# Full-row low products in the attention scores, and new byte positions for the token parts

## The chip, the cores and the metric

The kernel runs on one core of a Trainium2 chip. The metric is the device time of one execution in microseconds. Weights come from HBM, everything between stays in SBUF and PSUM.

## The reference

Two layers work on 512 tokens of 1024 channels: 256 latent tokens x and 256 context tokens ctx. Each layer is a feed-forward half, a token mixing and a second feed-forward half, each behind an RMS norm with shift and scale from a conditioning vector. In the second layer the context is needed only up to the keys and values of the mixing.

```
x = x + 0.5 * gate1 * SwiGLU(mod(rmsnorm(x)))            # ctx too; d_ff = 2816
x = x + gate2 * W_out( sum_b sigmoid(G_b) * P_b(branch_b) )   # ctx too in layer 0
x = x + 0.5 * gate3 * SwiGLU(mod(rmsnorm(x)))            # ctx too in layer 0
# branches of one input projection: A attention (4 heads, 2 key heads), B a gated
# linear recurrence in both directions, C pooled means, D attention in a 2-D window
# A and D:  s = q @ k.T / 8 ; p = softmax(s) ; o = p @ v      (head size 64)
```

All inputs and the result are float32.

## The kernel before

Tokens lie along the free dimension: `x` is a tile of 128 partitions by 8 chunks by 512 tokens (latents are columns 0 to 255, context 256 to 511).

**Products in parts.** A float32 product is made of three products of `fp32r` parts. A weight unit (128 x 1024) is loaded by SyncE as `raw`; ScalarE rounds it to `whi` (L74), VectorE takes the rest `wlo` (L77). The tokens are split the same way: `apply` (L346) writes the normed tokens as `xh` on ScalarE (L355) and `xl` on VectorE (L356), by way of a tile `nt` (L352). `mm3` (L94) then issues for each of 8 chunks k three matmuls into one PSUM bank: whi with xh (L102), whi with xl (L103), wlo with xh (L104); the weights are stationary and the tokens stream past. `group` (L106) does the same for several units at once. The hidden activations of a feed-forward half are parts `hh`, `hl`, the merged branches `mh`, `ml`, one branch `bh`, `bl`.

**Stages.** The program is one long list: feed-forward 1 of layer 0 (starts cold, `cold_units` L446), mixing of layer 0, feed-forward 2 of layer 0, feed-forward 1 of layer 1, mixing of layer 1, feed-forward 2 of layer 1. All products have 512 columns up to the mixing of layer 1, apart from the first units of a stage and the last two output units, which go in halves of 256 columns; from the mixing of layer 1 on nearly all have 256 columns. A unit of the gate and up projections (`pg`, `pu`) or of the mixing (`proj`, `gate`) is 24 matmuls, one of the down projection (`pd`) 33. The first units of a stage wait for `apply`; in the last stage `early_units` (L426) takes products of tokens that are not yet divided by their norm, kept in the context's half of `xh` (columns 256 to 511) with the shift in two columns more (512 and 513).

**Where the parts lie.** `xh` and `xl` are tiles of 8 x 514 columns (L146, L147), so chunk k starts 2056 bytes behind chunk k-1. In the compiled program xh starts at byte 36,032 of each partition and xl at 52,480: by lines of 128 bytes xh's chunk k starts at byte 64 + 8k of its line, xl's at byte 8k. `hh`, `hl` start at byte 64 of a line in every chunk (pitch 2048 bytes), `mh`, `ml` at byte 32 in layer 0 and 64 in layer 1. The weights start at byte 0 of a line in the pool that lasts (four buffers of `whi` and of `wlo`); units that a stage keeps in its own pool (the chunk c = 2 of a feed-forward half, the last two output units) lie at byte 64, in the mixing of layer 0 at byte 32.

**Scores.** `score_parts` (L637) makes for each of the two heads h of a pair a tile `qs` with the rounded q in the head's own 64 rows and again in the other 64, and `ks` with the rounded k in the own rows and its rest in the others. `attend` (L657) then needs two matmuls per head and 128 queries: qs with ks over 128 rows (L700), and for the rest of q, `ql`, over the head's own 64 rows (L701, one tile for both heads). 32 such pairs have 512 columns and 16 have 256. A tile framework orders the instructions of all generators and puts in the waits; on each engine they run in that order.

Of the kernel before, what the change touches and what calls it, by code (L numbers as in the profile page):

```python
# [17 lines left out]
P = 128  # L18
# [25 lines left out]
    0, 72, 80, 88, 96, 104, 105, 106, 107, 109, 117)  # L44

# [6 lines left out]
class Net:  # L52
# [41 lines left out]
    def mm3(self, ps, w, xh, xl, ks, c0, c1, first=True, last=True, k0=0):  # L94

        nc = self.nc
        hi, lo = w
        n = len(ks)
        for j, k in enumerate(ks):
            wh = hi[:, (k0 + j) * P:(k0 + j + 1) * P]  # L100
            wl = lo[:, (k0 + j) * P:(k0 + j + 1) * P]
            nc.tensor.matmul(ps, wh, xh[:, k, c0:c1], start=first and j == 0, stop=False)  # L102
            nc.tensor.matmul(ps, wh, xl[:, k, c0:c1], start=False, stop=False)  # L103
            nc.tensor.matmul(ps, wl, xh[:, k, c0:c1], start=False, stop=last and j == n - 1)  # L104

    def group(self, ws, pss, c0, c1, mid=iter(()), ks=range(NK), marks=(3, 5)):  # L106

        nc = self.nc
        for k in ks:
            if k in marks:  # L110
                next(mid, None)
            a, b = self.xh[:, k, c0:c1], self.xl[:, k, c0:c1]
            for (hi, lo), ps in zip(ws, pss):
                w = slice(k * P, (k + 1) * P)
                nc.tensor.matmul(ps, hi[:, w], a, start=k == 0, stop=False)
                nc.tensor.matmul(ps, lo[:, w], a, start=False, stop=False)
                nc.tensor.matmul(ps, hi[:, w], b, start=False, stop=k == NK - 1)
# [10 lines left out]
    def consts(self):  # L128
        nc, cp, i = self.nc, self.cp, self.i
        self.x = cp.tile([P, NK, TT], F32, name="x")  # L130
        self.cv = cp.tile([P, NK, 2], F32, name="cv")
# [14 lines left out]
        self.xh = cp.tile([P, NK, TT + 2], F32R, name="xh")  # L146
        self.xl = cp.tile([P, NK, TT + 2], F32R, name="xl")  # L147
# [13 lines left out]
        for k in range(NK):  # L161
            for r in range(2):
                sq = self.tp.tile([P, T], F32, tag="nt" if r else "sq", name="sq")
                x = self.x[:, k, r * T:(r + 1) * T]
                if r:
                    nc.vector.tensor_tensor(out=sq, in0=x, in1=x, op=ALU.mult)
                else:
                    nc.scalar.activation(sq, x, AF.Square)
                nc.tensor.matmul(ps[r], self.ones, sq, start=k == 0, stop=k == NK - 1)
        self.rstd = {r: self.tp.tile([P, T], F32, tag="rstd", name="rstd") for r in range(2)}  # L170
        for r in range(2):
            nc.scalar.activation(self.rstd[r], ps[r], AF.Sqrt, scale=1.0 / D, bias=self.eps)
            nc.vector.reciprocal(self.rstd[r], self.rstd[r])

# [17 lines left out]
    def bounds(self, pool):  # L192
# [4 lines left out]
        m = pool.tile([P, 4], F32, name="lbm")  # L197
# [148 lines left out]
    def apply(self, g, sh, r, ks=range(NK)):  # L346
# [21 lines left out]
    def early(self, l):  # L368
# [5 lines left out]
        hi = self.xh[:, :, TT:TT + 2]  # L374
        nc.scalar.copy(hi, sh)
        nc.vector.tensor_tensor(out=self.xl[:, :, TT:TT + 2], in0=sh, in1=hi.bitcast(F32), op=ALU.subtract)
# [49 lines left out]
    def early_units(self, ws, l, hp, hh, hl):  # L426
# [4 lines left out]
        self.group(ws, [p[:, :T + 2] for p in pss], T, TT + 2, self.stat_steps(0), marks=(1, 3))  # L431
        g = self.gain(l, 7, C_N2)
        self.apply(g, self.mods(l, 6), 0)
        for c in range(2):
            s, u = (hp.tile([P, TT], F32, tag="sg", bufs=2, name="sg") for _ in range(2))
            b = self.tp.tile([P, 2], F32, tag="eb", name="eb")
            for j, t in enumerate((s, u)):
                ps = pss[2 * c + j]
                nc.vector.tensor_copy(b[:, j:j + 1], ps[:, T:T + 1])
                nc.vector.tensor_tensor(out=t[:, :T], in0=ps[:, :T], in1=self.rstd[0], op=ALU.mult)  # L440
# [5 lines left out]
    def cold_units(self, wgu, hp, evac):  # L446
# [44 lines left out]
        hh, hl = (hp.tile([P, FH, TT], F32R, tag=t, name=t) for t in ("hh", "hl"))  # L491
# [5 lines left out]
    def ffn(self, l, wgu, wd, col, mods, segs, rate=0, whole=False, cold=False):  # L497
# [3 lines left out]
        gate = None  # L501
        with tc.tile_pool(name=f"ffn{col}_{l}", bufs=1) as hp:
            self.apool, self.rate = hp, rate
# [7 lines left out]
            for f in range(2):  # L511
                c = 0
                if cold and f == 0:
                    hh, hl = self.cold_units(wgu[l], hp, evac)
                    c = 2
                    self.steady = True
                else:
                    hh, hl = (hp.tile([P, FH, TT], F32R, tag=t, name=t) for t in ("hh", "hl"))
# [118 lines left out]
    def score_parts(self, pool, q, k, n, ks=None):  # L637
# [4 lines left out]
        ql = pool.tile([P, TT], F32R, tag="ql", name="ql")  # L642
# [3 lines left out]
        for h in range(2):  # L646
# [7 lines left out]
            nc.vector.tensor_tensor(out=ql[own, :n], in0=q[own, :n], in1=qs[h][own, :n].bitcast(F32), op=ALU.subtract)  # L654
        return qs, ql, ks

    def attend(self, pool, tmp, first, second, v, n, bias, bo):  # L657
# [7 lines left out]
        for i in range(len(items) + 2):  # L665
# [24 lines left out]
            if i < len(items):  # L690
# [5 lines left out]
                for h in range(2):  # L696
                    rows = slice(64 * h, 64 * h + 64)
# [3 lines left out]
                    nc.tensor.matmul(sc[:, :w], ql[rows, qc], ks[h][rows, k0:], start=False, stop=True)  # L701
# [111 lines left out]
    def mix(self, l, segs):  # L813
# [3 lines left out]
        cols = self.cols[l]  # L817
        with tc.tile_pool(name=f"mix{l}", bufs=1) as mp:
# [401 lines left out]
```

## Time and profile before

| | |
|---|---|
| median of 3 runs | 2163.44 us (2162.93 to 2164.12) |
| profiled execution | 2163.93 us, its span 2162.2 us |
| TensorE (PE) busy | 2140.1 us, 99%, 12446 matmul records |
| weight loads (PEld) | 1810.7 us, 84% |
| VectorE (DVE), ScalarE (ACT), GpSimd (POOL) | 66%, 42%, 2% |
| granted TensorE clock | 0.998 of 2.4 GHz |
| HBM | 136 GB/s over the span |

A matmul's row gives its start and a modelled length; consecutive matmuls overlap in it, so the pace is read from start to start, not from the length. A float32 matmul (not fp32r) has two records.

### The profile page before, as it was taken

To read this page: it belongs to the slowest core of one execution; us is meant where nothing else is said; L and a number is where in the kernel's file an instruction comes from. 1 tells how busy PE (TensorE), PEld (TensorE's weight loads), DVE (VectorE), ACT (ScalarE), POOL (GpSimd) and SP (SyncE) were. 2 spreads that over 40 slices of the span, in tenths; PEclk is the share of its full clock that TensorE was granted. 3 is DMA by queue.
4 is the path that set the end of the run, shared out by engine and by line. 5 is a ranking of instruction groups with operands and counts; after the bars stand their busy time and mean duration, and the time that the engine had idled before them with its cause. 6 is when DMAs were issued, how large, how long until landed. Compare 5 with 4: busy or idle time off the path is not lost.

```text
span 2162.2 us, 31602 instructions
## 1 busy us (share of the span) xinstructions
PE 2140.1 (99%) x12446; PEld 1810.7 (84%) x12446; DVE 1437.7 (66%) x2355; ACT 905.9 (42%) x1488; POOL 33.0 (2%) x79
## 2 busy tenths in 40 slices
PE   8999999999999999999999999999999999999998
PEld 5777777988787778888787888878789899999998
DVE  5987986676366454676676667567665867677555
ACT  4332333546446433433232344223334665656443
POOL 0000000000000000000000000000000000000000
PEclk9999999999999999999999999999999999999999
DMA  7655654221222222343454344445433233355553
GB/s 297 215 173 186 206 183 134 92 95 50 69 70 78 73 88 88 115 148 127 138 185 152 116 134 147 137 138 179 147 119 115 103 111 112 120 184 184 170 197 114
DMA packets 89509, 296.71 MB, mean 137 GB/s; under 512 B 10256, under 2 KB 12176, under 8 KB 89360
## 3 DMA queue, kind: packets, MB, share of 16 engines
q1 hardware_dynamic: 89360, 294.69, 40.3%
q8 instruction: 98, 1.61, 0.3%
q14 instruction: 51, 0.42, 0.1%
HBM read 293.60 MB, written 1.05 MB: 136 GB/s over the span
## 4 chain that ended last, share of the span: by engine, by line
PE 95%; DVE 2%; ACT 2%; issue 1%; DMA 0%; DVEq 0%; ACTq 0%; SPq 0%
PE pg L102 6%; PE pu L102 6%; PE pu L103 6%; PE pg L103 6%; PE pu L104 6%; PE pg L104 6%; PE pd L102 6%; PE pd L104 6%; PE pd L103 6%; PE gate L102 4%; PE gate L103 4%; PE gate L104 4%; PE proj L103 2%; PE proj L102 2%; PE proj L104 2%; PE blev L747 2%
## 5 line engine op out<-in xcount | busy, mean ns | idle before, releaser
L74 ACT CAST whi<-raw 128x1024 fp32r<-128x1024 f32 (+2 forms) x444 | 430.4, 972 | 907.1 <-PE pu L103 216.5
L77 DVE TENSOR_TENSOR wlo<-raw,whi 128x1024 fp32r<-128x1024 f32 (+2 forms) x444 | 498.6, 1124 | 331.0 <-ACT whi L74 327.6
L264 DVE SCALAR_TENSOR_TENSOR aacc<-araw,sil,aacc 128x512 f32<-128x512 f32 x448 | 312.4, 746 | 89.1 <-DMA araw<-in_wada 88.6
L102 PE MATMUL pg<-xh,whi 128*128 128x512 f32 (+1 forms) x640 | 235.4, 368 | 0.3 <-DVE sg L440 0.3
L102 PE MATMUL pu<-xh,whi 128*128 128x512 f32 (+1 forms) x640 | 235.1, 367 | 0.0
L103 PE MATMUL pu<-xl,whi 128*128 128x512 f32 (+1 forms) x640 | 235.0, 367 | 0.0
L103 PE MATMUL pg<-xl,whi 128*128 128x512 f32 (+1 forms) x640 | 234.9, 367 | 0.0
L104 PE MATMUL pu<-xh,wlo 128*128 128x512 f32 (+1 forms) x640 | 234.5, 366 | 0.0
L104 PE MATMUL pg<-xh,wlo 128*128 128x512 f32 (+1 forms) x640 | 234.5, 366 | 0.0
L102 PE MATMUL pd<-hh,whi 128*128 128x512 f32 (+1 forms) x616 | 226.4, 368 | 0.0
L104 PE MATMUL pd<-hh,wlo 128*128 128x512 f32 (+1 forms) x616 | 225.2, 366 | 0.0
L103 PE MATMUL pd<-hl,whi 128*128 128x512 f32 (+1 forms) x616 | 225.2, 366 | 0.0
L102 PE MATMUL gate<-xh,whi 128*128 128x512 f32 (+1 forms) x512 | 176.6, 345 | 0.0
L103 PE MATMUL gate<-xl,whi 128*128 128x512 f32 (+1 forms) x512 | 173.7, 339 | 0.0
L104 PE MATMUL gate<-xh,wlo 128*128 128x512 f32 (+1 forms) x512 | 173.4, 339 | 0.0
L102 PEld LDWEIGHTS pg<-xh,whi 128*128 128x128 f32 x640 | 120.6, 188 | 23.7 <-issue 2.0
L102 PEld LDWEIGHTS pu<-xh,whi 128*128 128x128 f32 x640 | 120.6, 188 | 23.2 <-issue 2.0
L104 PEld LDWEIGHTS pg<-xh,wlo 128*128 128x128 f32 x640 | 120.7, 189 | 20.9
L104 PEld LDWEIGHTS pu<-xh,wlo 128*128 128x128 f32 x640 | 120.7, 189 | 20.8
L103 PEld LDWEIGHTS pu<-xl,whi 128*128 128x128 f32 x640 | 120.5, 188 | 20.6
L103 PEld LDWEIGHTS pg<-xl,whi 128*128 128x128 f32 x640 | 120.5, 188 | 20.4
L102 PEld LDWEIGHTS pd<-hh,whi 128*128 128x128 f32 x616 | 115.7, 188 | 22.5 <-issue 2.2
(275 smaller groups left out, 3804.3 us busy)
## 6 DMA issues: line engine op xcount, KB each, us to landing
raw<-in_wgu SPq DMA_DIRECT2D x176, 512.0 KB, 3.3
araw<-in_wada SPq DMA_DIRECT2D x128, 512.0 KB, 3.2
raw<-in_wgate SPq DMA_DIRECT2D x64, 512.0 KB, 3.2
raw<-in_wd SPq DMA_DIRECT2D x64, 384.0 KB, 3.0
raw<-in_win SPq DMA_DIRECT2D x44, 512.0 KB, 3.3
raw<-in_wd SPq DMA_DIRECT2D x64, 320.0 KB, 2.8
aspace<-in_wada SPq DMA_DIRECT2D x16, 512.0 KB, 9.0
raw<-in_wbr SPq DMA_DIRECT2D x16, 512.0 KB, 3.4
```

The source lines that it names most:

```text
L74: nc.scalar.copy(hi, src)
L77: nc.vector.tensor_tensor(out=lo, in0=src, in1=hi.bitcast(F32), op=ALU.subtract)
L102: nc.tensor.matmul(ps, wh, xh[:, k, c0:c1], start=first and j == 0, stop=False)
L103: nc.tensor.matmul(ps, wh, xl[:, k, c0:c1], start=False, stop=False)
L104: nc.tensor.matmul(ps, wl, xh[:, k, c0:c1], start=False, stop=last and j == n - 1)
L264: nc.vector.scalar_tensor_tensor(out=acc[r], in0=w[:, j], scalar=c, in1=acc[r], op0=ALU.mult, op1=ALU.add)
L747: nc.tensor.matmul(ps[:, g * P:(g + 1) * P], k[:, h, g * P:(g + 1) * P], x[:, h, (g ^ cross) * P:((g ^ cross) + 1) * P], start=True, stop= ...
```

## The change

Four edits. (1) `xh` and `xl` become views of one tile `xs`; `place`, called at the head of each stage, sets them: 112 bytes into a line of 128 for both, 16,512 bytes apart, for the stages with 512 columns, and for the last two stages 64 bytes into a line, 18,432 bytes apart. The pitch of a chunk is 2048 bytes now. The two shift columns of `early_units` move into the last two columns of the latents' half. (2) `hidden` places `hh`, `hl` at byte 112 of a line (64 in the last stage), and a pad of 64 bytes heads the feed-forward pool. With it the weights that this pool holds move from byte 64 of a line to byte 0. `lbm` leaves the mixing's pool, whose tiles in layer 0 move from byte 32 to byte 0. (3) `ql` becomes one tile per head, its other 64 rows set to zero by GpSimd, and L701 runs over all 128 rows. (4) `nt` is one buffer of 512 columns, used in halves, in place of two of 256; the second `ql` lies in it too, and so do the squares of the context's half at the start.

```diff
+LINE = 32
+PLACES = {(0, C_N1): (28, NK * TT + LINE, (28, 12)), (0, C_NM): (28, NK * TT + LINE, None),
+          (0, C_N2): (28, NK * TT + LINE, (28, 12)), (1, C_N1): (28, NK * TT + LINE, (28, 12)),
+          (1, C_NM): (16, NK * TT + TT, None), (1, C_N2): (16, NK * TT + TT, (48, 0))}
...
+        self.xs = cp.tile([P, 2 * NK * TT + TT + LINE], F32R, name="xs")
-        self.xh = cp.tile([P, NK, TT + 2], F32R, name="xh")
-        self.xl = cp.tile([P, NK, TT + 2], F32R, name="xl")
...
-                sq = self.tp.tile([P, T], F32, tag="nt" if r else "sq", name="sq")
+                sq = self.tp.tile([P, TT], F32, tag="nt", bufs=1, name="sq")[:, :T] if r else self.tp.tile(
+                    [P, T], F32, tag="sq", name="sq")
...
+    def place(self, l, phase):
+        h, d, o = PLACES[l, phase]
+        self.xh, self.xl = (self.xs[:, a:a + NK * TT].rearrange("p (k t) -> p k t", t=TT) for a in (h, h + d))
+        return o
...
-        m = pool.tile([P, 4], F32, name="lbm")
+        m = self.tp.tile([P, 4], F32, tag="rs", name="lbm")
...
-        for k in ks:
-            t = self.tp.tile([P, T], F32, tag="nt", name="nt")
+        for j, k in enumerate(ks):
+            if j % 2 == 0:
+                pair = self.tp.tile([P, TT], F32, tag="nt", bufs=1, name="nt")
+            t = pair[:, j % 2 * T:j % 2 * T + T]
...
-        hi = self.xh[:, :, TT:TT + 2]
+        hi = self.xh[:, :, T - 2:T]
...
-        self.group(ws, [p[:, :T + 2] for p in pss], T, TT + 2, self.stat_steps(0), marks=(1, 3))
+        self.group(ws, [p[:, :T + 2] for p in pss], T - 2, TT, self.stat_steps(0), marks=(1, 3))
...
+    def hidden(self, hp, off):
+        return tuple(hp.tile([P, FH * TT + pad], F32R, tag=t, name=t)[:, a:a + FH * TT].rearrange(
+            "p (f t) -> p f t", t=TT) for t, pad, a in zip(("hh", "hl"), (48, 16), off))
...
+        off = self.place(l, col)
         with tc.tile_pool(name=f"ffn{col}_{l}", bufs=1) as hp:
+            hp.tile([P, LINE // 2], F32, name="pad")
...
-                    hh, hl = (hp.tile([P, FH, TT], F32R, tag=t, name=t) for t in ("hh", "hl"))
+                    hh, hl = self.hidden(hp, off)
...
-        ql = pool.tile([P, TT], F32R, tag="ql", name="ql")
+        ql = [pool.tile([P, TT], F32R, tag="ql", name="ql"), self.tp.tile([P, TT], F32R, tag="nt", bufs=1, name="ql")]
+        for h in range(2):
+            nc.gpsimd.memset(ql[h][64 - 64 * h:128 - 64 * h, :n].bitcast(F32), 0.0)
...
-                    nc.tensor.matmul(sc[:, :w], ql[rows, qc], ks[h][rows, k0:], start=False, stop=True)
+                    nc.tensor.matmul(sc[:, :w], ql[h][:, qc], ks[h][:, k0:], start=False, stop=True)
...
+        self.place(l, C_NM)
         with tc.tile_pool(name=f"mix{l}", bufs=1) as mp:
```

The edits in `mm3` and `group` name the same operands in another way and change no instruction.

## Rows read from the trace of the kernel before

**Rows 1.** The page: busy time of the matmul engine, and the chain by engine.

```profile
PE 2140.1 (99%) x12446; PEld 1810.7 (84%) x12446; DVE 1437.7 (66%) x2355; ACT 905.9 (42%) x1488; POOL 33.0 (2%) x79
...
PE 95%; DVE 2%; ACT 2%; issue 1%; DMA 0%; DVEq 0%; ACTq 0%; SPq 0%
```

**Rows 2.** Groups by line with shapes apart: shape, count, busy us, mean ns, idle before.

```profile
L102 PE MATMUL pg<-xh,whi 128*128 128x512 f32 x480 | 190.1, 396 | 0.0
...
L102 PE MATMUL pd<-hh,whi 128*128 128x512 f32 x462 | 183.9, 398 | 0.0
```

**Rows 3.** Timeline, PE, one unit of 512 columns: start us, length us, line, operation.

```profile
340.78 0.39 PE L102 MATMUL pu<-xh,whi 128*128 128x512 f32 x1
...
342.41 0.40 PE L103 MATMUL pu<-xl,whi 128*128 128x512 f32 x1
342.65 0.40 PE L104 MATMUL pu<-xh,wlo 128*128 128x512 f32 x1
...
344.98 0.39 PE L102 MATMUL pu<-xh,whi 128*128 128x512 f32 x1
...
345.67 0.39 PE L102 MATMUL pu<-xh,whi 128*128 128x512 f32 x1
...
346.13 0.39 PE L104 MATMUL pu<-xh,wlo 128*128 128x512 f32 x1
```

**Rows 4.** Timeline, PE, a down unit of 512 columns, first and last of 33.

```profile
354.60 0.40 PE L102 MATMUL pd<-hh,whi 128*128 128x512 f32 x1
...
362.07 0.40 PE L104 MATMUL pd<-hh,wlo 128*128 128x512 f32 x1
```

**Rows 5.** Timeline, PE, last stage, a down unit of 256 columns, first and last of 33.

```profile
2042.12 0.28 PE L102 MATMUL pd<-hh,whi 128*128 128x256 f32 x1
...
2045.75 0.28 PE L104 MATMUL pd<-hh,wlo 128*128 128x256 f32 x1
```

**Rows 6.** Timeline, PE, last stage, a unit with weights at byte 64, first and last of 33.

```profile
2143.01 0.28 PE L102 MATMUL last<-hh,whi 128*128 128x256 f32 x1
...
2146.85 0.28 PE L104 MATMUL last<-hh,wlo 128*128 128x256 f32 x1
```

**Rows 7.** Timeline, PE, output unit of the second mixing, first and 21st matmul.

```profile
1938.47 0.28 PE L102 MATMUL po<-mh,whi 128*128 128x256 f32 x1
...
1940.83 0.28 PE L104 MATMUL po<-mh,wlo 128*128 128x256 f32 x1
```

**Rows 8.** Timeline, PE, units of 256 columns, first and last of 24: gate, then pu.

```profile
1899.35 0.28 PE L102 MATMUL gate<-xh,whi 128*128 128x256 f32 x1
...
1902.07 0.28 PE L104 MATMUL gate<-xh,wlo 128*128 128x256 f32 x1
...
2018.47 0.29 PE L102 MATMUL pu<-xh,whi 128*128 128x256 f32 x1
...
2021.24 0.28 PE L104 MATMUL pu<-xh,wlo 128*128 128x256 f32 x1
```

**Rows 9.** Timeline, PE, a score pair of 512 columns and what follows it.

```profile
496.52 0.48 PE L700 MATMUL s<-ks,qs 128*128 128x512 f32 x1
496.93 0.50 PE L701 MATMUL s<-ks,ql 64*128 64x512 f32 x1
497.37 0.50 PE L102 MATMUL gate<-xh,whi 128*128 128x512 f32 x1
```

**Rows 10.** Groups by line with shapes apart, GpSimd.

```profile
L738 POOL MEMSET bqz<- 64x512 f32 x32 | 17.0, 531 | 580.4 <-DVE xl L356 368.5 <-PE blev L747 149.1 <-PE bo L808 35.0
```

**Rows 11.** Timeline, VectorE, the last square of the start.

```profile
13.04 0.43 DVE L166 TENSOR_TENSOR sq<-x 128x256 f32<-128x256 f32 x1 [0.44 <-PE stat L169]
```

**Rows 12.** Timeline around the end of `early_units`: VectorE's pairs of chunks, PE's next unit.

```profile
1971.91 0.87 DVE L352 SCALAR_TENSOR_TENSOR nt<-x,gain,rstd 128x256 f32<-128x256 f32 x2
...
1973.77 0.88 DVE L352 SCALAR_TENSOR_TENSOR nt<-x,gain,rstd 128x256 f32<-128x256 f32 x2
...
1975.19 0.36 PE L102 MATMUL pg<-xh,whi 128*128 128x256 f32 x1 [0.26 <-DVE sg L440]
```

More of the change, by code (lines that the diff above doesn't have):

```diff
@@ L101, in mm3 @@
             wl = lo[:, (k0 + j) * P:(k0 + j + 1) * P]
-            nc.tensor.matmul(ps, wh, xh[:, k, c0:c1], start=first and j == 0, stop=False)
-            nc.tensor.matmul(ps, wh, xl[:, k, c0:c1], start=False, stop=False)
-            nc.tensor.matmul(ps, wl, xh[:, k, c0:c1], start=False, stop=last and j == n - 1)
+            a, b = xh[:, k, c0:c1], xl[:, k, c0:c1]
+            nc.tensor.matmul(ps, wh, a, start=first and j == 0, stop=False)
+            nc.tensor.matmul(ps, wh, b, start=False, stop=False)
+            nc.tensor.matmul(ps, wl, a, start=False, stop=last and j == n - 1)
     def group(self, ws, pss, c0, c1, mid=iter(()), ks=range(NK), marks=(3, 5)):
@@ L113, in group @@
             for (hi, lo), ps in zip(ws, pss):
[L114 to L117, printed above, removed]
+                wh, wl = hi[:, k * P:(k + 1) * P], lo[:, k * P:(k + 1) * P]
+                nc.tensor.matmul(ps, wh, a, start=k == 0, stop=False)
+                nc.tensor.matmul(ps, wl, a, start=False, stop=False)
+                nc.tensor.matmul(ps, wh, b, start=False, stop=k == NK - 1)
     def warm(self, func, after):
@@ L373, in early @@
         sh = self.mods(l, 6)
-        hi = self.xh[:, :, TT:TT + 2]
+        hi = self.xh[:, :, T - 2:T]
         nc.scalar.copy(hi, sh)
-        nc.vector.tensor_tensor(out=self.xl[:, :, TT:TT + 2], in0=sh, in1=hi.bitcast(F32), op=ALU.subtract)
+        nc.vector.tensor_tensor(out=self.xl[:, :, T - 2:T], in0=sh, in1=hi.bitcast(F32), op=ALU.subtract)
         return g
@@ L438, in early_units @@
                 ps = pss[2 * c + j]
[L439 to L440 removed]
+                nc.vector.tensor_copy(b[:, j:j + 1], ps[:, 0:1])
+                nc.vector.tensor_tensor(out=t[:, :T], in0=ps[:, 2:T + 2], in1=self.rstd[0], op=ALU.mult)
             nc.scalar.activation(s[:, :T], s[:, :T], AF.Silu, bias=b[:, 0:1])
@@ L513, in ffn @@
                 if cold and f == 0:
-                    hh, hl = self.cold_units(wgu[l], hp, evac)
+                    hh, hl = self.cold_units(wgu[l], hp, evac, off)
                     c = 2
@@ L517, in ffn @@
                 else:
-                    hh, hl = (hp.tile([P, FH, TT], F32R, tag=t, name=t) for t in ("hh", "hl"))
+                    hh, hl = self.hidden(hp, off)
                 while c < FH:
@@ L653, in score_parts @@
                 nc.vector.tensor_tensor(out=ks[h][other], in0=k[own], in1=ks[h][own].bitcast(F32), op=ALU.subtract)
-            nc.vector.tensor_tensor(out=ql[own, :n], in0=q[own, :n], in1=qs[h][own, :n].bitcast(F32), op=ALU.subtract)
+            nc.vector.tensor_tensor(out=ql[h][own, :n], in0=q[own, :n], in1=qs[h][own, :n].bitcast(F32), op=ALU.subtract)
         return qs, ql, ks
```

3 lines of the change are left out of this document (1 added, 2 removed).

## The prediction

> **What bounds the kernel now.** I read the page first: the matmul engine is busy 99% of the span, and the chain that ended last runs through it for 95% [rows 1]. So the time is a sum of paces: so many products, each by the distance from its start to the next one's start. The length in a row is no pace: the 512-column products of [rows 2] have a mean length of 396 to 398 ns and overlap. I then read paces from the timeline, unit by unit, and set each beside the byte at which its operands start (the section on the kernel gives the bytes). The reader is to see five of them.
>
> - 512 columns of token parts: first to last of 24 in 5.35 us, 23 steps, 232.6 ns [rows 3]. Inside the unit the steps differ. Chunk 6 (xh at byte 112, xl at 48) takes 0.69 us for its three, 230 ns each; the step that begins with xl at byte 16 takes 0.24 us.
> - 512 columns of hidden parts, all at byte 64: 7.47 us for 32 steps, 233.4 ns [rows 4].
> - 256 columns of hidden parts, all at byte 64, weights at byte 0: 3.63 us for 32 steps, 113.4 ns [rows 5]. The same parts with weights at byte 64: 3.84 us, 120.0 ns [rows 6].
> - 256 columns of merged parts, again 64 and 0: 2.36 us for 20 steps, 118.0 ns [rows 7]. So one placement can run at two paces, 113.4 and 118.0.
> - 256 columns of token parts, bytes changing with the chunk: gate 2.72 us for 23 steps, 118.3 ns; pu 2.77 us, 120.4 ns [rows 8].
>
> The last place to read is the scores. From the start of a full-row product to that of its half-row partner pass 0.41 us, and from there to the next product 0.44 us [rows 9], where two ordinary 512-column products would take 0.47.
>
> **The change part by part.** The sum is made against the profiled execution's 2163.93 us (span 2162.2 and 1.7 around it), which is 0.5 above the median.
>
> *Token parts of 512 columns at byte 112.* By the code 24 products a unit: 120 gate and up units with 24 each (2880, six times the 480 of [rows 2]), four cold units (96), 32 gate units and 15 projections of the first mixing (768 and 360): 4104. No row has both parts at 112. The nearest is chunk 6 of [rows 3], 230 ns among neighbours at other bytes. Below it I set twice the 113.4 of [rows 5], 226.8 ns, as the floor: the smallest pace that a steady run of equal bytes shows, doubled for twice the columns. Above it stands 233.4 [rows 4], a steady run of 512 columns at byte 64. I take 227.5, near the floor, since in [rows 5] the steady run is below every mixed one of [rows 8], and chunk 6 is the lowest part of the mixed unit. 4104 x (232.6 - 227.5) = 20.9 us; ends 23.8 and -3.3.
>
> *Hidden parts of 512 columns at byte 112.* 462 products a line [rows 2] by three lines, 1386. 1386 x (233.4 - 227.5) = 8.2 us; ends 9.1 and 0.
>
> *Weights of the stage's pool at byte 0.* 396 output products of the three wide halves (12 units by 33), 120.0 now [rows 6], then 256 columns at byte 112 between 113.4 and 118.0; with 116: 1.6 us (0.8 to 2.6). 66 of the last stage go to 113.4: 0.4. 96 of the first mixing: 0.3 (0 to 0.6).
>
> *Token parts of 256 columns at byte 64.* They then lie as the hidden parts of [rows 5] and the merged parts of [rows 7] do, in lines and in weights; the distance between the parts is a multiple of 2048 bytes in all three. So 113.4 or 118.0. Last stage: 1056 products (44 units of 24), 120.4 now [rows 8]; undisturbed, so I take 114.5: 6.2 us (2.5 to 7.4). Second mixing: 1104 products (32 gate, 9 projection and 5 first units), 118.3 now; attention breaks in between, 115.5: 3.1 us (0.3 to 5.4). Halves in the earlier stages, 528 at byte 112, 118.3 to 116: 1.2 us (0 to 2.6). 144 products of 512 columns in the second mixing go to 233.4: -0.1.
>
> A rule speaks against these three parts. The Trainium skill, "TensorE: Matmul & The Clock Gate", section "Step-by-step: what each phase is for", says that the engine reads weights and streaming operand through two independent ports, so that loading the next weights takes nothing from the running product. By it the bytes would not matter. This trace disagrees: the same hidden parts run at 113.4 or 120.0 ns with the weights alone moved [rows 5, 6]. What the rule would give is a rival below.
>
> *Full-row low products.* A pair costs 0.85 us now [rows 9] and two like products then 0.47: 0.38 us. The code has 32 pairs of 512 columns and 16 of 256; what is exposed is not the streaming, so I use 0.38 for all: 48 x 0.38 = 18.2 us at most. The lower end is the half-row product's own excess, 0.44 - 0.23, by 48: 10. I take 16, for some of the time saved will be spent in waits on softmax that the engine meets sooner. What it costs: 16 zero fills on GpSimd of the size of [rows 10], 0.53 us each, on an engine that is busy 2% [rows 1]. They run beside ScalarE's copies of q into qs, which wait for the same score products to free their buffers. Behind them on GpSimd stand the recurrence's zero fills of [rows 10]; if each were late by 0.53 us and PE waited for it, 8.5 us would go.
>
> The same page of the Trainium skill, section "The mechanism" (of row and column tiling), says that a weight load runs ahead of a running product only where the row groups differ. By it the half-row products of the two heads could run beside each other, and full rows would lose that. The row shows the reverse: 0.41 and 0.44 us on either side of the half-row product [rows 9], nothing beside it.
>
> *One `nt` buffer.* `apply` works in pairs of chunks (x2 in [rows 12]): two nt, two xh, two xl, then the next two, whose VectorE writes stand in order behind the xl of the pair before. One buffer of two halves keeps that order: 0. At the start the context's squares lose their second buffer. Each of eight then waits for PE and takes its 0.43 us [rows 11] where it ran ahead: 3.4 us at most; PE has the latents' square to work on meanwhile and later waits for loads, so I take 0.5.
>
> *Shift columns in the latents' half.* `apply` now overwrites columns that `early_units` still reads, so chunk k waits for the products of chunk k. `apply` writes two chunks per 1.86 us [rows 12], and its last pair is written when the group is ending anyway: 0. If the wait were for the whole group, four pairs would stand in line behind it, 7.4 us, before PE's next unit at 1975.19.
>
> Sum: 20.9 + 8.2 + 1.6 + 0.4 + 0.3 + 6.2 + 3.1 + 1.2 - 0.1 + 16 - 0.5 = 57.3 us. 2163.9 - 57.3 = 2106.6; on the median's footing 2106.
>
> **The rivals.**
> - *512 columns keep the steady 233.4 at any byte* [rows 4]. For it: 64 and 32 are the only bytes with long steady runs of that width, and the former shows this pace. Against: chunk 6 of [rows 3]. The first two terms become -3.3 and 0, the rest stays 28.2: 2139.
> - *The byte does nothing at all,* as the ports rule would have it; only scores and start remain, 15.5 us: 2148. Against: [rows 5, 6].
> - *The scores' time turns into waits* for softmax or the recurrence. For it: DVE and ACT are busy 66% and 42% on the whole [rows 1] and the recurrence is a serial chain through them. Against: PE's chain is 95% its own. 57.3 - 16: 2123.
> - *Byte 112 locks into a slow pattern.* [rows 5] and [rows 7] show that equal bytes run in a steady pattern that repeats, good or bad; a byte can show 0.24 us in one step [rows 3]. At 240 ns for all 512-column products the first two terms turn into 4104 x 7.4 + 1386 x 6.6 = 39.5 us lost, against 28.2 won elsewhere: slower, 2175. It decides from 5.1 ns above today's mean of 232.8, that is from 237.9 ns (28.2 us by 5490 products).
> - *The parts don't lie where it says.* xs must start at a line of 128 bytes; by the compiled program x starts at byte 16,512 and takes 16,384, so xs follows at a line. Were it off, the first rival's time would hold.
>
> **How the numbers follow.** Forecast 0.66, steady 233.4 (and parts misplaced) 0.14, no effect of the byte 0.05, scores into waits 0.08, slow pattern 0.07. All terms at their good end are worth 70 us: 2093; a pace under the floor would go below. The range 2088 to 2142 takes in the forecast, the waits and the steady 233.4 and leaves out the other two, 0.12, and some of the tails. Changes under 0.2% (4.3 us) can't be told from none here. Faster 0.93 (all but the slow pattern), within 0.2% 0.01, slower 0.06.
>
> **What would show it.** A pu unit of the first stages with 23 steps in 5.23 us (227.5) in place of 5.35, and a down unit with 32 in 7.28; in the last stage pu in 2.63; the last output units at 113.4 in place of 120.0; score pairs 0.47 from first start to the next product, all on 128 rows; nothing new in PE's waits at 1975. Wrong would be: units at 233 or more, score pairs followed by idle PE, or a gap before the first unit behind `early_units`.

## The result, and the profile after

The changed kernel takes 2151.8 us in the median of four executions (2145.98 to 2152.58) against 2163.31: ratio 0.994, interval 0.9923 to 0.9958. It is faster by 11.5 us where 57 were forecast, and outside the range. The profiled execution took 2152.58 us, its span 2150.8, 11.4 under the span before. One execution of experiment 1 ran at a mean granted clock of 0.594, took 3530.24 us, and is left out below.

Line numbers have moved: `mm3` is L110 to L112 (was L102 to L104), scores L724 and L725, `apply` L368 to L372. The page after; the rows of before are [rows 1].

```profile
PE 2117.5 (98%) x12446; PEld 1809.5 (84%) x12446; DVE 1440.8 (67%) x2355; ACT 904.6 (42%) x1488; POOL 39.5 (2%) x95
...
PE 94%; DVE 3%; ACT 2%; issue 1%; DMA 0%; DVEq 0%; ACTq 0%; SPq 0%
```

PE's busy time fell by 22.6 us, but the span by 11.4: PE now stands idle where it did not. The paces are read from start to start, as before. First come a down unit of 512 columns in the second feed-forward (to be set beside [rows 4]) and a pu unit of 512 columns of the same stage (beside [rows 3]).

```profile
1086.53 0.39 PE L110 MATMUL pd<-hh,whi 128*128 128x512 f32 x1
...
1093.78 0.39 PE L112 MATMUL pd<-hh,wlo 128*128 128x512 f32 x1
...
1122.64 0.40 PE L110 MATMUL pu<-xs,whi 128*128 128x512 f32 x1
...
1128.04 0.39 PE L112 MATMUL pu<-xs,wlo 128*128 128x512 f32 x1
```

The down unit takes 7.25 us for 32 steps, 226.6 ns: the forecast's floor. The pu unit takes 5.40 for 23, 234.8 ns, more than the 232.6 before. Both kinds of part start at byte 112 of a line. In blocks of 256 bytes they do not lie alike: xs starts at byte 32,896, so xh lies at 33,008, byte 240 of 256, and xl at 49,520, byte 112. `hh` lies at 132,208, byte 112, and `hl` at 154,864, byte 240. From here on, "240/112" names the byte of the high and the low part in a block of 256.

A score pair ([rows 9]): 0.31 us to the low product and 0.23 from there, 0.54 where it was 0.85.

```profile
495.60 0.48 PE L724 MATMUL s<-ks,qs 128*128 128x512 f32 x1
495.91 0.39 PE L725 MATMUL s<-ks,ql 128*128 128x512 f32 x1
496.14 0.39 PE L724 MATMUL s<-ks,qs 128*128 128x512 f32 x1
```

In the last stage, at 192/192, pu and pd units run at 2.71 us for 23 steps and 3.77 for 32, both 117.8 ns. Before, the pu units were at 120.4 ([rows 8]) and the pd units at 113.4, with the same bytes as now ([rows 5]).

```profile
1990.27 0.28 PE L110 MATMUL pu<-xs,whi 128*128 128x256 f32 x1
...
1992.98 0.28 PE L112 MATMUL pu<-xs,wlo 128*128 128x256 f32 x1
...
2015.71 0.28 PE L110 MATMUL pd<-hh,whi 128*128 128x256 f32 x1
...
2019.48 0.28 PE L112 MATMUL pd<-hh,wlo 128*128 128x256 f32 x1
```

The largest single loss is at the start. PE's waits (engine, line, what it waited for: us in total, times, longest):

```profile
PE mm L123 <- ACT xs L371: 8.2, 3, 5.1
...
PE s L724 <- ACT bad L802: 1.8, 4, 0.7
...
PE pt L711 <- ACT ap L736: 1.5, 2, 1.2
```

The first was 2.6 us before. VectorE's timeline shows why: after the change one chunk at a time, scale (L368), a wait for ScalarE's copy, subtract (L372), then the next.

```profile
34.91 0.48 DVE L368 SCALAR_TENSOR_TENSOR nt<-x,gain,rstd 128x256 f32<-128x256 f32 x1
35.97 0.48 DVE L372 SCALAR_TENSOR_TENSOR xs<-nt,mod,xs 128x256 fp32r<-128x256 f32 x1 [0.58 <-ACT xs L371]
36.49 0.48 DVE L368 SCALAR_TENSOR_TENSOR nt<-x,gain,rstd 128x256 f32<-128x256 f32 x1
...
65.26 0.68 DVE L531 TENSOR_TENSOR sg<-sg,mm 128x512 f32<-128x512 f32 x1
```

The same place before, two at a time:

```profile
30.73 0.88 DVE L352 SCALAR_TENSOR_TENSOR nt<-x,gain,rstd 128x256 f32<-128x256 f32 x2
31.79 0.89 DVE L356 SCALAR_TENSOR_TENSOR xl<-nt,mod,xh 128x256 fp32r<-128x256 f32 x2 [0.18 <-ACT xh L355]
...
55.24 0.68 DVE L508 TENSOR_TENSOR sg<-sg,mm 128x512 f32<-128x512 f32 x1
```

The first hidden chunk is made at 65.26 us, before at 55.24: 10.0 us. PE's longest idle time, 5.14 us before 57.98, brings a second cost: its granted clock. Windows of the changed kernel (us from:to, length, busy of PE, PEld, DVE, ACT, POOL, granted clock, DMA share, GB/s):

```profile
52.00:55.00 3.00, 0.84 (x4) 0.36 (x2) 3.00 (x9) 0.51 (x1) 0.00 (x0) 1.00 0.42 134
55.00:57.00 2.00, 0.00 (x0) 0.00 (x0) 2.00 (x4) 0.00 (x0) 0.00 (x0) 0.89 0.41 131
57.00:63.30 6.30, 5.32 (x13) 4.16 (x14) 6.30 (x13) 2.64 (x4) 0.00 (x0) 0.50 0.57 196
```

After that idle time the work goes on at 0.50, 1.2 GHz, until about 63 us; before the change the clock was 1.00 (2.4 GHz) there. The 12 steps from 57.98 to 63.27 us take 5.29 us, where 512-column products go at 0.23 us each behind them: about 2.5 us, an estimate, are lost by the clock. It stood at 0.50 once before, from 25.9 to 29.2 us, behind an idle time of 2.30 us.

Where the 11.4 us come from, as sums of start-to-start times by stage and kind: scores -14.5, hidden parts of 512 columns -8.3, merged and branch parts of the first mixing -1.9, second mixing -2.0, token parts of the last stage -2.3, weights of the stage's pool -0.8; against them the start +10.0, token parts of 512 columns +4.0, hidden parts of the last stage +1.9, waits on softmax +1.0, early units +0.8. That makes -12.1, 0.7 more than the span shows; the rest is spread over small groups.

### The profile page after: what moved, and what is told of

Its sections match the earlier page's. It is cut to its first block, busy times and chain, and to the rows that moved or that the text cites. A ratio compares the mean times of both kernels' runs of the same rounds, so it can differ in the third digit from the quotient of the medians.

```text
span 2150.8 us, 31652 instructions
## 1 busy us (share of the span) xinstructions
PE 2117.5 (98%) x12446; PEld 1809.5 (84%) x12446; DVE 1440.8 (67%) x2355; ACT 904.6 (42%) x1488; POOL 39.5 (2%) x95
## 4 chain that ended last, share of the span: by engine, by line
PE 94%; DVE 3%; ACT 2%; issue 1%; DMA 0%; DVEq 0%; ACTq 0%; SPq 0%
PE pg L110 6%; PE pu L110 6%; PE pu L112 6%; PE pg L112 6%; PE pu L111 6%; PE pg L111 6%; PE pd L110 6%; PE pd L112 6%; PE pd L111 6%; PE gate L110 4%; PE gate L112 4%; PE gate L111 4%; PE proj L110 2%; PE proj L111 2%; PE proj L112 2%; PE blev L771 2%
## 5 line engine op out<-in xcount | busy, mean ns | idle before, releaser
L110 PE MATMUL pg<-xs,whi 128*128 128x512 f32 (+1 forms) x640 | 238.0, 372 | 0.8 <-DVE sg L456 0.8
L110 PE MATMUL pu<-xs,whi 128*128 128x512 f32 (+1 forms) x640 | 237.9, 372 | 0.0
L111 PE MATMUL pu<-xs,whi 128*128 128x512 f32 (+1 forms) x640 | 235.1, 367 | 0.0
L111 PE MATMUL pg<-xs,whi 128*128 128x512 f32 (+1 forms) x640 | 235.1, 367 | 0.0
L112 PE MATMUL pg<-xs,wlo 128*128 128x512 f32 (+1 forms) x640 | 234.8, 367 | 0.0
L112 PE MATMUL pu<-xs,wlo 128*128 128x512 f32 (+1 forms) x640 | 234.8, 367 | 0.0
L112 PE MATMUL pd<-hh,wlo 128*128 128x512 f32 (+1 forms) x616 | 224.3, 364 | 0.0
L110 PE MATMUL pd<-hh,whi 128*128 128x512 f32 (+1 forms) x616 | 223.8, 363 | 0.0
L110 PE MATMUL gate<-xs,whi 128*128 128x512 f32 (+1 forms) x512 | 175.0, 342 | 0.0
L112 PE MATMUL gate<-xs,wlo 128*128 128x512 f32 (+1 forms) x512 | 173.0, 338 | 0.0
L111 PE MATMUL gate<-xs,whi 128*128 128x512 f32 (+1 forms) x512 | 172.2, 336 | 0.0
L110 PEld LDWEIGHTS pg<-xs,whi 128*128 128x128 f32 x640 | 120.9, 189 | 23.4 <-issue 2.0
L112 PEld LDWEIGHTS pu<-xs,wlo 128*128 128x128 f32 x640 | 121.4, 190 | 22.2
L112 PEld LDWEIGHTS pg<-xs,wlo 128*128 128x128 f32 x640 | 121.4, 190 | 22.2
L110 PEld LDWEIGHTS pu<-xs,whi 128*128 128x128 f32 x640 | 120.9, 189 | 22.3 <-issue 2.0
L111 PEld LDWEIGHTS pu<-xs,whi 128*128 128x128 f32 x640 | 121.2, 189 | 21.0
L111 PEld LDWEIGHTS pg<-xs,whi 128*128 128x128 f32 x640 | 121.2, 189 | 20.8
L110 PEld LDWEIGHTS pd<-hh,whi 128*128 128x128 f32 x616 | 116.3, 189 | 19.5 <-issue 2.2
```

The source lines that it names most:

```text
L110: nc.tensor.matmul(ps, wh, a, start=first and j == 0, stop=False)
L111: nc.tensor.matmul(ps, wh, b, start=False, stop=False)
L112: nc.tensor.matmul(ps, wl, a, start=False, stop=last and j == n - 1)
```

## The experiments

**1. The chains of the cold start.** In `cold_units`, `apply` is called with one chunk, and each call takes a whole pair buffer. The edit hands it one half of a shared buffer; the part of the edit inside `apply`, which uses that half, is not shown.

```diff
...
             for k in (2 * j, 2 * j + 1):
+                pair = self.tp.tile([P, TT], F32, tag="nt", bufs=1, name="nt")
                 for r in range(2):
-                    self.apply(gain, mod, r, (k,))
+                    self.apply(gain, mod, r, (k,), pair[:, r * T:r * T + T])
```

> The changed kernel with one edit in cold_units: the two halves of one nt tile go to r = 0 and r = 1 of the same chunk, so that the two chains of scale, copy and subtract overlap as in the kernel before. Theory A (each one-chunk apply takes a whole pair buffer, so the chains stand in line and the first stage starts late): the pairs come back as nt x2 and xs x2 on VectorE, the first evacuation (65.26 us after the change, 55.24 before) comes at 56 to 57.5, 1.5 us of the old gap staying with the squares, and the run is 7.5 to 9 us under the changed kernel's 2151.8: 2143 to 2144.5. Rival B (the start is late because of loads or of the weight splits that share VectorE): the evacuation stays at 64 to 65 and the time within 2 us of 2151.8.

Measured: 2138.34, 2143.78 and 2144.93 us, ratio 0.9896 (0.9876 to 0.9915). Profile against profile, both with the last stage at 117.8 ns, 2143.78 against 2152.58: 8.8 us. VectorE's timeline:

```profile
32.57 0.88 DVE L369 SCALAR_TENSOR_TENSOR nt<-x,gain,rstd 128x256 f32<-128x256 f32 x2
33.63 0.88 DVE L373 SCALAR_TENSOR_TENSOR xs<-nt,mod,xs 128x256 fp32r<-128x256 f32 x2 [0.18 <-ACT xs L372]
...
57.73 0.68 DVE L533 TENSOR_TENSOR sg<-sg,mm 128x512 f32<-128x512 f32 x1
```

The pairs are back and PE's wait for xs is 1.4 us in place of 8.2. Theory A holds; the first hidden chunk, at 57.73, is still 2.5 late, and the clock's fall behind 57 us is gone.

**2. The token parts 128 bytes further, and both at byte 0.** In `PLACES`, for the four stages with 512 columns, from 240/112 to 112/240; the other kernel has `(32, NK * TT, ` there, 0/0:

```diff
-PLACES = {(0, C_N1): (28, NK * TT + LINE, (28, 12)), (0, C_NM): (28, NK * TT + LINE, None),
+PLACES = {(0, C_N1): (60, NK * TT + LINE, (28, 12)), (0, C_NM): (60, NK * TT + LINE, None),
...
```

> The changed kernel with one number changed: in the four wide stages the token parts start 128 bytes later in xs. The high part goes from byte 240 to byte 112 of a 256-byte block and the low part from 112 to 240, the distance of 129 lines of 128 bytes stays. Theory A (the pace hangs on which half of a 256-byte block the part used by two of three products starts in; the hidden parts, high at 112 and low at 240, run at 226.6 ns): the 512-column units of token parts go from 234.6 ns to 226.6 to 228; about 3000 products of the three FFNs by 7.5 ns and 1100 of the first mixing by 5.5 make 28 us, so 2123 to 2125. Rival B (the distance between the parts decides, 177 lines in the hidden parts): they stay at 234.6 and the time at 2151 to 2153. Rival C (eight chunks and 24 products against eleven and 33 make the pattern): stays too.

> The changed kernel with the token parts of the four wide stages both at byte 0 of a 256-byte block, 128 lines apart, as the merged parts of the first mixing lie (226.7 ns). Theory A (the half of the 256-byte block of the high part decides): 226.7 to 228 ns in the 512-column units, 2123 to 2125, like the run with the parts swapped; the 256-column products may move between 113.4 and 118. Rival B (the distance of 129 lines is what is slow): 226.7 here too, and not in the run with the parts swapped. Rival C (units of 24 products lock at 234.6 whatever the byte): 2151 to 2153.

Measured: 2121.64 us, ratio 0.9809 (0.9794 to 0.9824), and 2123.22, 0.9811 (0.9795 to 0.9827). PE's timeline, a pu unit of the second feed-forward; parts swapped:

```profile
924.76 0.39 PE L110 MATMUL pu<-xs,whi 128*128 128x512 f32 x1
...
929.97 0.39 PE L112 MATMUL pu<-xs,wlo 128*128 128x512 f32 x1
```

Both at 0:

```profile
923.90 0.39 PE L110 MATMUL pu<-xs,whi 128*128 128x512 f32 x1
...
929.12 0.39 PE L112 MATMUL pu<-xs,wlo 128*128 128x512 f32 x1
```

5.21 and 5.22 us for 23 steps, 226.5 and 227.0 ns. So neither the distance of 129 lines nor the 24 products make the 234.6; in the first kernel a move of both parts by 128 bytes, which leaves the byte in a line of 128 as it is, does away with it. Profile against profile at like levels of the last stage (experiment 5), the swap gave 24.6 us (2152.58 to 2127.95): 24.5 of it in the token parts of 512 columns, the rest in small gains and losses that nearly cancel. I had worked out 28.

**3. A map of bytes.** Two kernels give every stage other bytes (the pads of `hh` and `hl` grow to 64 columns each):

```diff
+PLACES = {(0, C_N1): (60, NK * TT, (0, 0)), (0, C_NM): (0, NK * TT, None),
+          (0, C_N2): (28, NK * TT, (60, 28)), (1, C_N1): (0, NK * TT + 32, (28, 28)), ...
```

> The changed kernel with another pair of bytes in every stage (byte of the high and of the low part in a block of 256, lines whole multiples of 2048 apart but for the third wide feed-forward), to be read unit by unit. Token parts of 512 columns: first feed-forward 112 and 112, first mixing 128 and 128, second feed-forward 240 and 240, third 128 and 0. Hidden parts: 0 and 0, 240 and 112, 112 and 112. Theory A (the high part, used by two products of three, must start in the lower half of the block): 226.6 to 228 ns for 112/112, 0/0 and 112/112 again, 233 to 235 for 128/128, 240/240, 240/112 and 128/0. Rival B (what counts is that the parts lie in the order lower half, upper half, or both at 0): 112/112 slow too. Rival C (the number of products in a unit decides, 33 against 24): the hidden parts stay at 226.6 everywhere. Last stage, 256 columns, all at 64 of 256: 113.3 or 117.8 if the line's byte is all that counts there. By A the time is near 2147, by C near 2144.

> As the map before, with other bytes. Token parts of 512 columns: first feed-forward 64 and 64, first mixing 32 and 32, second feed-forward 0 and 128, third 16 and 16. Hidden parts: 128 and 128, 240 and 240, 16 and 16. Theory A (lower half of the 256-byte block for the high part): 226.6 to 228 for 64/64, 0/128 and 16/16, 233 to 235 for 128/128 and 240/240; the merged parts at 32/32 in the kernel before ran at 233.4, so 32/32 is expected slow, which A alone doesn't explain. Rival B (only the byte in the 128-byte line counts, 0 and 112 being good): 128/128 and 240/240 fast, which the 234.6 at 240/112 after the change speaks against. Last stage, 256 columns, all at 128: 113.3, 117.8 or 120. By A the time is near 2137.

They took 2152.43 and 2157.7 us, in one execution each; what counts are the units. Mean pace in ns of the units of a stage with 512 columns (the step at a unit's head, which holds its waits, is left out; another cut there moves a figure by up to 0.2):

| high/low | token parts | hidden parts |
|---|---|---|
| 0/0 | 227.0 | 227.1 |
| 112/240 | 227.2 | 227.2 (after) |
| 128/0 | 229.0 | |
| 64/64 | 229.3 | |
| 112/112 | 230.9 | 231.1 |
| 16/16 | 231.7 | 231.7 |
| 128/128 | 232.3 | 232.6 |
| 0/128 | 232.9 | |
| 32/32 | 233.2 | |
| 192/192 | | 233.3 (before) |
| 240/112 | 234.2 (after) | 234.0 |
| 240/240 | 236.1 | 236.6 |

The two ends of the map in rows: 240/240, a pu unit of the first map (5.44 us for 23 steps, 236.5 ns), and a down unit of the second (7.57 for 32, 236.6).

```profile
967.84 0.40 PE L110 MATMUL pu<-xs,whi 128*128 128x512 f32 x1
...
973.28 0.40 PE L112 MATMUL pu<-xs,wlo 128*128 128x512 f32 x1
```

```profile
1047.08 0.40 PE L110 MATMUL pd<-hh,whi 128*128 128x512 f32 x1
...
1054.65 0.40 PE L112 MATMUL pd<-hh,wlo 128*128 128x512 f32 x1
```

Seven placements were seen in both kinds of unit, at different addresses, distances and counts of products, and agree within 0.5 ns: the two bytes in a block of 256 set the mean pace of a stage. A block of 512 is not needed: in one, the two 0/0 cases lie at 256/256 (33,024 and 49,408) and 0/256 (132,096 and 154,880), and their paces are 227.0 and 227.1.

The bytes do not settle the pace alone, which the means hide. In the second map the first three whole units at 64/64 run at 233.3 ns; behind a break, short products of another kind (`ada`) between two units, all later ones of the stage run at 229.0. The third unit, the break, and the fifth, 5.37 and 5.26 us for 23 steps:

```profile
76.29 0.40 PE L110 MATMUL pg<-xs,whi 128*128 128x512 f32 x1
...
81.66 0.39 PE L112 MATMUL pg<-xs,wlo 128*128 128x512 f32 x1
81.98 0.43 PE L290 MATMUL ada<-afold,pick 128*32 128x128 f32 x8
...
87.95 0.39 PE L110 MATMUL pg<-xs,whi 128*128 128x512 f32 x1
...
93.21 0.39 PE L112 MATMUL pg<-xs,wlo 128*128 128x512 f32 x1
```

At 240/240 the same kind of break turned the token units from 233.3 to 236.6. At 240/112 the changed kernel has both 231.1 (half of the first mixing's whole units) and 234.3, steady steps taken alone. At 0/0, 112/240, 112/112 and 128/0 every steady run of these kernels was seen at one pace (226.7, 226.7, 231.1 and 228.9).

Theory A fell all the same. The high part's half does not decide: 128/0 is fast, 0/128 slow. Where both parts share a byte, 128 more costs 4 to 6 ns (0/0, 64/64, 112/112); otherwise what the low part does depends on the high one. I have a table and no rule. In the last stage, with 256 columns, the maps gave 117.8 ns at 64/64 and 118.7 at 128/128.

**4. The scores alone.** The kernel before with this edit only:

```diff
-        ql = pool.tile([P, TT], F32R, tag="ql", name="ql")
+        ql = [pool.tile([P, TT], F32R, tag=f"ql{h}", name="ql") for h in range(2)]
+        for h in range(2):
+            nc.gpsimd.memset(ql[h][64 - 64 * h:128 - 64 * h, :n].bitcast(F32), 0.0)
...
-  ... ql[rows, qc], ks[h][rows, k0:] ...
+  ... ql[h][:, qc], ks[h][:, k0:] ...
```

> The kernel before with the full-row low products of the scores alone, each head with its own ql in the mixing stage's pool; every other operand at the byte where it was. Theory A (full rows take away the exposed weight loads on both sides): the steps 0.31 and 0.43 us become 0.12 and 0.23, 14 to 15 us in all, 2163.3 - 14.5 = 2149. Rival B (the time turns into waits on softmax and the recurrence): under 8 us, 2155 or more, with idle time of the matmul engine in both mixings. The forecast had 16.

Measured: 2149.11 us, ratio 0.9931 (0.9916 to 0.9945), 14.8 us under the 2163.91 beside it. Theory A holds in the total; this pair's first step went to 0.32 us and not to the 0.12 expected. PE's timeline, 0.32 and 0.23 us:

```profile
495.04 0.48 PE L701 MATMUL s<-ks,qs 128*128 128x512 f32 x1
495.36 0.39 PE L702 MATMUL s<-ks,ql 128*128 128x512 f32 x1
495.59 0.39 PE L102 MATMUL gate<-xh,whi 128*128 128x512 f32 x1
```

The rows of the weight loads (PEld) of a `ql` product, before and with this edit, show where the time was:

```profile
496.93 0.18 PEld L701 LDWEIGHTS s<-ks,ql 64*128 64x128 f32 x1 [0.25 <-issue]
```

```profile
495.13 0.19 PEld L702 LDWEIGHTS s<-ks,ql 128*128 128x128 f32 x1
```

Before, the load starts at 496.93, only with its own product ([rows 9]); with full rows it starts at 495.13, 0.23 us ahead of its product at 495.36.

This small part alone gives more than the whole change in the median: the rest of the change cost about 3 us net there (11.5 won against 14.8). In the changed kernel's fastest execution, 2145.98, by its time on the lower of the two levels of experiment 5, the rest won about 3.

**5. The three edits together, and the last stage's two levels.** Both at 0, the shared pair, and the context's squares at the start in halves of a pair (in the expectation they are called the latents'; it is the context's half that uses `nt`):

```diff
         for k in range(NK):
+            if k % 2 == 0:
+                pair = self.tp.tile([P, TT], F32, tag="nt", bufs=1, name="sq")
             for r in range(2):
-                sq = self.tp.tile([P, TT], F32, tag="nt", bufs=1, name="sq")[:, :T] if r else ...
+                sq = pair[:, k % 2 * T:k % 2 * T + T] if r else ...
```

> The changed kernel with three edits: token parts of the four wide stages both at byte 0 of a 256-byte block, the pair of nt halves shared by r = 0 and r = 1 of a chunk in cold_units, and the latents' squares at the start in the halves of a pair too, two of them in flight. Theory A (the three losses add up): 28 from the bytes, 8.8 from the chains, 1 to 1.5 from the squares, so the first evacuation at 55.5 to 56.5 us and 2151.8 - 38 = 2114, or 7 less where the last stage runs at 113.3 in place of 117.8 ns. Rival B (the start is bounded by loads once the chains overlap): the squares give nothing, the evacuation stays at 57.7, and 2115.5.

Measured: 2110.72 us, ratio 0.9766 (0.9748 to 0.9784). The first hidden chunk comes at 55.48, 2.25 earlier than with the shared pair alone; from the profile with both at 0 (2120.67) to this one (2110.06) are 10.6 us, 8.8 of them the chains and so, by difference, 1.8 the squares. Small shares are uncertain: kernels with the same start as before have their first hidden chunk 0.7 us apart (55.24 before, 54.55 with the scores alone).

```profile
55.48 0.68 DVE L534 TENSOR_TENSOR sg<-sg,mm 128x512 f32<-128x512 f32 x1
```

Its four executions lie at 2110.06, 2110.51, 2110.94 and at 2117.1. So do those of all kernels with the last stage at 192/192: 12 at a lower and 12 at a higher level, between 5 and 8 us apart. The profiles show what that is: where the lower level was profiled (both at 0, the three edits), the last stage's pu and pd units run at 113.3 ns, otherwise at 117.8; 1056 + 528 products by 4.5 ns make 7.1 us, an estimate. Other bytes there:

> The three-edit version (2110.7 us) with other bytes in the second mixing and the last stage, where products have 256 columns: token parts at 192 and 64 of 256 (16,512 bytes apart), hidden parts at 112 and 112. The state of affairs: at 192 and 192 a run of units sits at 113.3 or at 117.8 ns, and executions of one kernel lie some 7 us apart (2110 and 2117). Theory A (some bytes hold 113.3 whatever came before, as 0/0 and 112/240 hold 226.6 with 512 columns): the last stage at 113.3 to 114 in every execution, all four times within 1.5 us of each other near 2109 to 2110. Rival B (no byte does): 117 to 120 in one of the two kinds of part, 2114 to 2120. I lean to B for the hidden parts, which ran at 113.3 to 118.6 at 112/112 in the earlier stages' last units.

> As the run with 192/64, with token parts of the second mixing and the last stage at 112 and 112 and hidden parts at 160 and 160. Theory A (some bytes hold 113.3): one of the two kinds of part at 113.3 to 114 in the profile; with both, four times near 2110. Rival B: 115 to 120, 2113 to 2120. With 512 columns 112/112 ran at 230.9, twice 115.4, so 115.4 for the token parts would say that a row of 256 costs half a row of 512 at the same bytes.

Measured: 2114.95 to 2115.64 (median 2115.53), tokens at 192/64 117.9 ns, hidden parts at 112/112 113.6; and 2111.45 to 2113.20 (2112.31), tokens at 112/112 113.4, hidden parts at 160/160 117.3. In each only one kind is slow, and no second level shows. I had leaned to the wrong side for the hidden parts. Then everything there at 112/112 (hidden pads of 64 columns):

```diff
-          (1, C_NM): (16, NK * TT + TT, None), (1, C_N2): (16, NK * TT + TT, (48, 0))}
+          (1, C_NM): (60, NK * TT, None), (1, C_N2): (60, NK * TT, (28, 28))}
```

> The three-edit version without a break, with token parts and hidden parts of the last stage, and token parts of the second mixing, all at byte 112 of 256. Each kind alone ran at 113.3 to 113.6 in the last stage. Theory A (112/112 with 256 columns holds 113.3 whatever came before): six executions within 1.5 us at 2109.5 to 2111. Rival B (two paces there too): executions some 5 to 7 us apart, or at 115 to 118.6 in the profile, as the last units of the earlier stages show it.

And, at 192/192, breaks (one fp32 product of 128 columns each) ahead of all gate units of the last stage; one break (the condition with `and f == 0 and c == 3`); and one that reads a hidden part:

```diff
+                    if len(segs) == 1:
+                        self.keep_warm(1)
...
+                    if len(segs) == 1 and f == 0 and c == 5:
+                        wm = self.ps.tile([P, TT], F32, tag="ada", bufs=1, name="warm")
+                        nc.tensor.matmul(wm[:, :P], self.ones, hh[:, 3, :P].bitcast(F32), start=True, stop=True)
```

> The three-edit version with one fp32 product of 128 columns into an unused bank ahead of each of the 20 gate units of the last stage. Theory A (at 192/192 the pace is chosen where a steady run is entered and then stays; a break chooses anew): in one execution some gate units at 113.3 and some at 117.8, the unit behind taking the pace of the one ahead, and times of the four executions closer together than 7 us. Rival B (the pace belongs to the whole execution, set by something outside the stage): all units of the stage at one pace, times 7 us apart. The products themselves cost about 20 x 0.2 to 0.3 = 4 to 6 us, so 2115 to 2122.

> The three-edit version with one fp32 product of 128 columns into an unused bank, ahead of the second gate unit of the last stage only. With 20 of them every unit fell to 113.3 ns and four executions lay within 2.1 us. Theory A (such a break leads the run behind it to 113.3 whatever pace it had, and it then stays): all executions within 1.5 us of each other at 2110 to 2111.5, the break costing 139 + 94 ns. Rival B (the entries of that run were 113.3 by luck, the break chooses anew): executions at two levels again, near 2110.5 and 2117.

> The three-edit version (last stage at 192/192) with one fp32 product of 128 columns that reads a hidden part of two units before, so that it stands between the third and the fourth gate unit of the last stage; the one break of the run before was issued in the second mixing, far ahead of the stage. Theory A (a break of this kind leads the run behind it to 113.3 ns whatever pace it had, and it then stays): units behind the product at 113.3 in the profile, and all executions within 2 us, at 2109.5 to 2112: three units at 117.8 ahead of it cost at most 0.7 us. Rival B (a break chooses anew, or does nothing): executions at two levels some 6 us apart, as in the kernels with 192/192 and no break (2110 and 2117).

Measured: all at 112/112, 2109.2 us, ratio 0.9745 (0.9732 to 0.9758), the best version, four executions between 2108.05 and 2110.62, more apart than the 1.5 expected but on one level. A pu unit there takes 2.61 us for 23 steps, 113.5 ns:

```profile
1931.61 0.28 PE L110 MATMUL pu<-xs,whi 128*128 128x256 f32 x1
...
1934.22 0.28 PE L112 MATMUL pu<-xs,wlo 128*128 128x256 f32 x1
```

Breaks ahead of the gate units: 2114.0, four between 2113.43 and 2115.56, all units at 113.3 past their head; neither theory had that. The one break was a miss: the framework issued the product at 1865.27, in the second mixing, over 60 us ahead of the unit it was meant for, and the stage's units then ran at 117.8; five executions at two levels, 2109.3 and 2110.78 against 2116.58 to 2117.42.

```profile
1865.27 0.38 PE L194 MATMUL warm<-ones 128*128 128x128 f32 x2
...
1931.66 0.28 PE L110 MATMUL pu<-xs,whi 128*128 128x256 f32 x1
...
1934.37 0.28 PE L112 MATMUL pu<-xs,wlo 128*128 128x256 f32 x1
```

The break held in the stage stands where it should:

```profile
1945.46 0.38 PE L563 MATMUL warm<-hh,ones 128*128 128x128 f32 x2
1945.60 0.37 PE L110 MATMUL pg<-xs,whi 128*128 128x256 f32 x1
```

2110.49 us, five executions between 2109.17 and 2110.72. With a break inside the stage nine executions of nine are on the lower level, without one 12 of 24. That speaks for a state that a break enters anew. In this stage no profile caught a run at 117.8 turned by a break (the units ahead of it were at 113.3 too). In the second mixing, where the token parts lie at 192/192 as well, the pace changes at breaks both ways, though branch products at other bytes stand between the units there: in the changed kernel the gate unit at 1888.61 us runs at 117.8, the proj unit at 1892.82, right behind products of another kind (`hstat`), at 113.4, and the gate units from 1906.22, behind a wait, at 117.8 again. So a break does not always lead to the fast pace, and what picks the level where a run is entered stays open. At 112/112 it matters less: in the second mixing of the best version whole gate units that begin with steps of 114 to 130 ns all end at 113 or 114.

## Why the prediction was wrong, point by point

- **Token parts of 512 columns, 20.9 us: failed.** The step was "I take 227.5, near the floor", with places told by the byte in a line of 128. The pace hangs on the byte in a block of 256, and by lines the two kinds of part looked alike while their high parts lay at 240 and at 112. They went to 234.2 and lost 4.0 us; experiment 2 got 24.5 back by moving them 128 bytes. The prediction had the addresses, divided them by 128 and went no further; in the kernel before, the byte moves by 8 from chunk to chunk, so that no unit of token parts shows a placement by itself. Chunk 6, on which it leaned, has its high part at byte 240 of 256 (36,032 + 6 x 2056 = 48,368), not at 112. The rival "slow pattern" named the mechanism for all 512-column products; it came for three quarters of them, and weaker (234.2 against the 240 assumed).
- **Hidden parts, 8.2 us: right** (8.3), by luck of the block: 112/240 is one of the two fastest placements of the map.
- **One `nt` buffer, 0: failed.** The step was "`apply` works in pairs of chunks". That holds where it runs over eight chunks; in `cold_units` each call has one chunk, and the pair of before was r = 0 with r = 1. Experiment 1 gives 8.8 us for it. In it are the chains in line, the other work that slips in between their links on VectorE, and the time at 1.2 GHz behind PE's idle time, some 2.5 us by the estimate above; no run separates the shares. The squares, put at 0.5 (3.4 at most), measured 1.8.
- **Scores, 16: nearly right.** 14.5 in the pairs, 14.8 as the sole edit; 1.0 went into softmax waits, as the smaller term of 16 allowed.
- **Last stage, 6.2: failed in size.** The prediction saw that one placement can run at 113.4 and 118.0, and then took a value near the lower. In the profiled execution the tokens gained 2.3 and the hidden parts, left at their bytes and given no term, lost 1.9: the step that failed is "undisturbed, so I take 114.5". Undisturbed, the whole stage holds one of two levels, 113.3 or 117.8, and of the 24 executions half are on each. That the hidden parts were held at 113.4 before by token units with changing bytes ahead of them is a guess.
- **Second mixing, 3.1:** 2.0 with the branch and merged parts. **Weights of the stage's pool, 2.3:** 0.8, the units going to 117.7 and not to 116 in the wide stages, and to 117.8 and not to 113.4 in the last. **Halves in the earlier stages, 1.2:** about nothing. **First mixing's merged and branch parts,** which left byte 32 for byte 0, were not in the sum: 1.9.
- **Shift columns, 0:** early units +0.8, and the pg unit behind them waits 0.81 us, was 0.26 ([rows 12]); the rival of the whole group's 7.4 did not come.

```profile
1964.76 0.36 PE L110 MATMUL pg<-xs,whi 128*128 128x256 f32 x1 [0.81 <-DVE sg L456]
```

The rival "the byte does nothing" gave 2148, near the result by accident: gains and losses of the bytes cancelled. The rule of the Trainium skill behind it, "TensorE: Matmul & The Clock Gate", section "Step-by-step: what each phase is for", has weights and streaming operand come through ports of their own, and the prediction read from it that no byte would matter. That reading went too far. What the map shows, the streaming operand's bytes alone moving 512 columns from 227.0 to 236.6 ns, is neither for nor against two ports; [rows 5, 6], where the weights alone moved, are the rows here that bear on them.

## What to carry to other kernels

Read a pace against the whole address, in blocks at least as large as the structure that you suspect, and place high and low parts by a map that was measured, since no one byte decides. When two buffers become one of two halves, look at every caller: those that ask for a single piece take the whole buffer and lose the overlap. Take the parts of a change apart before the sum is trusted: here one of them was worth 14.8 us and the rest, as placed, about nothing (3 us lost in the median, 3 won in the fastest execution), while with other bytes and its buffers mended it brought 40 more (2149.1 to 2109.2). Prefer bytes at which only one pace was ever seen.

## What the runs showed of the hardware that was not expected

With equal bytes a steady run can hold either of two paces inside one execution, and a break can turn it. Experiment 3 has this for 512 columns; here are 256. Gate units of the second mixing, changed kernel, both at 192/192: 2.61 us and 2.71 us for 23 steps, 113.5 and 117.8 ns.

```profile
1763.51 0.28 PE L110 MATMUL gate<-xs,whi 128*128 128x256 f32 x1
...
1766.12 0.28 PE L112 MATMUL gate<-xs,wlo 128*128 128x256 f32 x1
...
1867.41 0.28 PE L110 MATMUL gate<-xs,whi 128*128 128x256 f32 x1
...
1870.12 0.28 PE L112 MATMUL gate<-xs,wlo 128*128 128x256 f32 x1
```

Good bytes are not the same for both widths: 0/0 is the best with 512 columns (227.0) and among the worst with 256 (the first map's output units of the first feed-forward, hidden parts at 0/0: 120.0).
